# Low parts of weights made by an adding DMA instead of a VectorE subtraction, in a planned one-core residual block

## The chip, the cores and the metric

The kernel runs on one core of one Trainium2 chip. A core has a matrix engine (TensorE, "PE" in the profile, with its weight loads listed apart as "PEld"), VectorE ("DVE"), ScalarE ("ACT"), GpSimd ("POOL") and SyncE ("SP"). They run their own instruction queues, each in order, and wait for one another through semaphores; 16 DMA engines move data between the chip's memory and the core's SBUF. The metric is the device time of one execution in microseconds, the median of the runs.

## What is computed

One block of a hybrid encoder on a sequence of 1024 tokens of width 1024, all in float32. Cut to what matters:

```python
h = rms_norm(x, norm_mix_pre)
proj = h @ w_in                                # 1024 x 5376 weights
q, k, v = heads(proj[..., :1536])              # stick-breaking attention, 8 heads of 64
o_sb = stick_breaking_attention(q, k, v)
o_rw = rwkv7_time_mix(proj[..., 1536:3328])    # RWKV-7: token shift, LoRA, scan over time
gates = sigmoid(proj[..., 3328:] + b_gate)
merged = gates[..., :D] * (o_sb @ w_sb_out) + gates[..., D:] * (o_rw @ w_rw_out)
x = x + rms_norm(merged @ w_o, norm_mix_post)
h = rms_norm(x, norm_ffn_pre)
f = (silu(h @ w_ffn_gate) * (h @ w_ffn_up)) @ w_ffn_down
out = x + rms_norm(f, norm_ffn_post)
```

## The kernel before

**Products in three parts.** Large products run in a float32 format of PE that keeps fewer bits than float32 (`fp32r` in the profile). To keep the precision, each operand is split into a high part, which is the operand rounded to that format, and a low part, which is what the rounding left. A product is then high x high + high x low + low x high, three matmuls that add into one PSUM tile (`mm3`, line 606). For each block of 128 rows of the contraction the order is: weight high with activation high, weight high with activation low, weight low with activation high. So the low part of a weight is needed by the third matmul of its product.

**How a weight tile is made.** `weights` (line 599) loads a tile into a place of class `raw` with a DMA of SP's queue (`load`, line 589), takes a place each of classes `whi` and `wlo` (`parts`, line 594), and splits (`split`, line 602): ACT copies `raw` to the high part in the rounded format, and DVE subtracts the high part from `raw` into the low part. The classes `raw`, `whi` and `wlo` have two places each (lines 665 and 666), so that one tile can be prepared while another is in use. `split` also serves activations and the later stages; these call it without `weights`.

**Who calls `weights`.** `rwkv` (line 900) for 12 tiles of `w_in`; `gate_tiles` (line 799) for 16; `att_inputs` (lines 1187, 1198, 1214) for 12; `merge` (line 1308) for 16 tiles of `w_sb` and `w_rw`, half as large. The first 40 have 128 x 1024 elements and feed two products of 24 matmuls each (two halves of the sequence), the 16 have 128 x 512 and feed two of 12. The two tiles of `w_in` for the LoRA stage and those of `w_o` and the FFN are split elsewhere.

**Stages.** `norm_in` normalises and transposes the input, `lora` computes the small projections and spills three arrays per pair of heads, `rwkv` runs four pairs of heads in two halves each: elementwise work, an inversion of small triangular blocks on DVE (`rw_inverse`, a series of 31 steps), and a chain of 8 steps (`rw_chain`) in which PE, DVE, ACT and POOL take turns; POOL makes the tile `sp` of each step. `attention` runs 8 heads, with a mask by POOL, a scan by DVE and transposes by PE. `merge` multiplies with the output weights and the gates, which were spilled to memory and are loaded again (`b_mg`). `output` and `ffn` follow. Projections of later pairs and the gate tiles are filler work for PE: they have no partner that waits soon.

**The planner.** Nothing is issued as it is written. Every operation is recorded (`record`, line 321) with a cost in ns (`cost`, line 132) and with what it reads and writes, and `schedule` (line 414) then plays the machine: five engines, each taking the able operation of highest priority as soon as it is free, places of SBUF and PSUM granted in turn, and a delay from each operation to those that depend on it (`LATENCY`, line 248; 2030 ns and more after a DMA of SP). An operation's `late` (ns) is added to that delay. The order that comes out is issued engine by engine, and on the chip each engine keeps to it. So a change of one cost can move instructions on every engine.

**Issue.** In the profile nearly all instructions have line 586, where the planned operations are issued, so groups are told apart by their tiles: `whi_whi<-raw_raw` is the copy to the high part, `wlo_wlo<-raw_raw,whi_whi` the subtraction, `d_d<-big_h,whi_whi` a matmul of a projection into the PSUM class `d`. All DMAs go out on SP's queue. In a row of the profile a place taken over by another tile of its class can lend it its name (`b_sh`, `b_dg`, ...).

Of the kernel before, what the change touches and what calls it, by code (L numbers as in the profile page):

```python
# [7 lines left out]
F32R = mybir.dt.float32r  # L8
BF16 = mybir.dt.bfloat16
AF = mybir.ActivationFunctionType  # L10
ALU = mybir.AluOpType
# [5 lines left out]
S = 1024  # L17
# [62 lines left out]
def is_ap(x):  # L80
    return hasattr(x, "tensor") and hasattr(x, "offset") and hasattr(x, "ap")


def count(shape):
    n = 1
    for d in shape:
        n *= d
    return n
# [43 lines left out]
def cost(engine, method, kw, in_psum):  # L132

    out = kw.get("out", kw.get("ap"))
    if out is None:
        return 1283.0
    n = count(out.shape[1:])
    if engine == "tensor":
        if method == "transpose":
            return 2 + max(out.shape[0], n) / 1.2  # L140
        m, full = count(kw["lhsT"].shape[1:]), kw["lhsT"].dtype == F32
        if out.shape[0] <= CH and n <= CH:
            return 65.0 if out.shape[0] == CH else 20.0
        return 2 * (2 + max(m, n) / 1.2) if full else max(m / 2.4, 1.5 + 0.4435 * n)
    psum = any(is_ap(v) and k not in OUTS and in_psum(v) for k, v in kw.items())
    if engine == "vector":
        if method == "tensor_copy" and not psum:
            return 60 + 0.52 * n
        if method == "tensor_reduce":
            n = count(kw["in_"].shape[1:])  # L150
            return 64 + 1.042 * n
        if method == "scalar_tensor_tensor":
            return max(196, 68 + (1.16 if psum else 1.1) * n)
        if method == "tensor_tensor_scan":
            return 60 + 2.083 * n
        if method == "tensor_tensor" and abs(kw["in0"].ap[-1][0]) > 16:
            return 68 + 1.8 * n
        return 68 + 1.042 * n
    if engine == "scalar":
        extra = "accum_out" in kw or any(is_ap(kw.get(k)) for k in ("scale", "bias"))  # L160
        return 55 + 0.833 * n + (0 if psum else 40) + (90 if extra else 0)
    if engine == "gpsimd":
        if method == "memset":
            return 98 + 0.8 * n
        if method == "tensor_copy":
            return 180 + 3.4 * n
        if method == "tensor_scalar":
            return 320 + 2.4 * n
        return 150 + 2.1 * n
    size = 4 * count(out.shape)  # L170
    return max(450.0, size / 360.0)

SHORT_RUNS = 2200.0


HELD, HEAD = 115.0, 140.0
# [84 lines left out]
class Block:  # L263
# [54 lines left out]
    def in_psum(self, ap):  # L318
        return not str(ap.space).endswith("DRAM") and self.tiles[ap.offset // TSTRIDE - 1].cls.psum
# [277 lines left out]
        return hi, lo  # L597

    def weights(self, src, shape):
        return self.parts(self.load(src, shape), shape)  # L600

    def split(self, hi, lo, src):
        self.nc.scalar.copy(hi, src)
# [45 lines left out]
def hybrid_block(tc, x, xt, w_in, consts, params, rows, ups, gup, w_sb, w_rw, w_o, w_fg, w_fu, w_fd, out):  # L649
    b = Block(tc, {a.tensor.name for a in (x, xt, w_in, consts, params, rows, ups, gup, w_sb, w_rw, w_o, w_fg, w_fu, w_fd)})  # L650
    nc = b
    T = b.t
    with ExitStack() as es:
        b.open(es)
        b.cls("cst", 1, CC_TI)
        b.cls("par", 1, PC_N)
        b.cls("small", 4, 16)
        b.cls("tiny", 4, 4)
        b.cls("ss", 8, 4)
        b.cls("carry", 5, 1)  # L660
        b.cls("pl", 3, 8)
        b.cls("sp", 3, CH)
        b.cls("q", 4, 256)
        b.cls("big", 4, 4 * S)
        for n in ("raw", "whi", "wlo"):
            b.cls(n, 2, S)
        b.cls("b", NB, 1040, halves=True)
        for n, k in (("d", 2), ("e", 2), ("c", 2), ("y", 2)):
            b.cls(n, k, H, psum=True)

        cst, par = T("cst", [P, CC_TI]), T("par", [P, PC_N])

        one = T("q", [P, P])
        nc.gpsimd.memset(one, 1.0)
        b.zero = T("b", [P, H], BF16, "zero")
        nc.vector.memset(b.zero, 0.0)
        idle_products(b, AWAKE[0])

        b.xin, b.w_lora, b.xt = [], [], []
        def tokens(*ms):  # L680
            for m in ms:
                b.xin.append(T("b", [P, D], F32, "x"))
                nc.sync.dma_start(b.xin[m], x[m * P : m * P + P, :])
        def channels(t):
            for q in range(2):
                b.xt.append(T("b", [P, 4, TQ], F32, "xt"))
                nc.sync.dma_start(b.xt[-1], xt[t][:, 4 * q : 4 * q + 4, :])
        tokens(0)
        nc.sync.dma_start(cst[:, 0:P], consts[:, 0:P])
        tokens(1)  # L690
        nc.sync.dma_start(par, params)
        b.w_lora.append(b.load(w_in[24], [P, KT, P]))
        channels(0)
        b.w_lora.append(b.load(w_in[25], [P, KT, P]))
        tokens(2, 3)
        channels(1)
        tokens(4, 5)
        nc.sync.dma_start(cst[:, P:CC_TI], consts[:, P:CC_TI])
        channels(2)
        tokens(6, 7)  # L700
        channels(3)
        b.ident = cst[:, CC_ID : CC_ID + P]
        b.cen = cst[:, CC_CEN : CC_CEN + P]
        b.ones = cst[:, CC_ONE : CC_ONE + P]
        b.mask_a = cst[:, CC_MA : CC_MA + P]
        b.tinit = consts[:, CC_TI : CC_TI + 256]
        b.scanm = consts[:, CC_SC:CC_N]
        b.eps = T("small", [P, 2])
        nc.gpsimd.memset(b.eps[:, 0:1], RMS_EPS)
        nc.gpsimd.memset(b.eps[:, 1:2], GN_EPS)  # L710
        b.om = T("small", [P, 14])
        nc.gpsimd.tensor_scalar(out=b.om, in0=par[:, PC_MU : PC_MU + 14], scalar1=-1.0, scalar2=1.0, op0=ALU.mult, op1=ALU.add)
        b.oka = T("small", [P, 4])
        nc.gpsimd.tensor_scalar(out=b.oka, in0=par[:, PC_KA : PC_KA + 4], scalar1=-1.0, scalar2=1.0, op0=ALU.mult, op1=ALU.add)
        b.pc = lambda col: par[:, col : col + 1]

        b.gsc = [b.scratch([P, S], f"gsc{j}") for j in range(16)]
        b.orw_d = [b.scratch([P, S], f"orw{p}") for p in range(PAIRS)]
        b.x2_d = b.scratch([S, D], "x2d")
        b.w_in, b.w_sb, b.w_rw = w_in, w_sb, w_rw  # L720
        b.ngate = 0

        b.steady = STEADY[0]
        norm_in(b, one)
        lora(b, ups, gup)
        b.steady = STEADY[1]
        rwkv(b)
        b.steady = STEADY[2]
        attention(b)
        b.steady = STEADY[3]  # L730
        ms, sums = merge(b)
        b.steady = True
        output(b, x, w_o, rows, ms, sums)
        ffn(b, w_fg, w_fu, w_fd, rows, out)
        b.issue()


def idle_products(b, n, after=None):
    ps = b.t("y", [P, H])
    for i in range(n):  # L740
        b.tensor.matmul(ps, lhsT=b.zero[:, 0:P], rhs=b.zero, start=True, stop=True)
        if after:
            b.ops[-1].preds.add(after)
# [150 lines left out]
def rwkv(b):  # L894
    T = b.t
    b.table("natural_log_exp_and_others")
    carry = {}
    units = [[{}, {}] for p in range(PAIRS)]

    def project(p):  # L900
        for name, j in (("k", 4 + p), ("r", p), ("v", 8 + p)):
            w = b.weights(b.w_in[12 + j], [P, KT, P])
            for hf in range(2):
                ps = b.proj(w, hf)
                units[p][hf][name] = T("b", [P, H], F32, name)
                shifted(b, ps, carry, j, hf, units[p][hf][name])

    project(0)
    for p in range(PAIRS):
        for hf in range(2):  # L910
            rw_elementwise(b, units[p][hf], p, hf, b.spill[p][hf])
        if p + 1 < PAIRS:
            with Offset(b, PROJ):
                project(p + 1)
        gate_tiles(b, GATES_R[p])
        with Offset(b, CHAIN):
            for hf in range(2):
                rw_chain(b, units[p], p, hf)
                with Offset(b, POST):
                    rw_post(b, units[p][hf], p, hf, b.spill[p][hf])  # L920


def rw_elementwise(b, u, p, hf, spill):
# [95 lines left out]
    for at in ((hi, slice(None), lo), (lo, slice(None), hi)):  # L1019
        nc.sync.dma_start(xv[at], sv[at])  # L1020
        b.ops[-1].late = SHORT_RUNS

# [28 lines left out]
def rw_inverse(b, nd, nx, quads, tinit, p, hf):  # L1051
# [22 lines left out]
    nc.sync.dma_start(dt[:], td.rearrange("(c a) j k t -> (a j k) c t", a=4))  # L1074
    b.ops[-1].late = SHORT_RUNS

# [376 lines left out]
def ffn(b, w_fg, w_fu, w_fd, rows, out):  # L1453
    b.act = b.scratch([7, NFF // 2, P, H], "act")
    ffn_up(b, w_fg, w_fu)
    ffn_down(b, w_fd, rows, out)
# [324 lines left out]
```

## Time and profile before

| | us |
|---|---|
| median of 3 runs | 1591.97 |
| lowest and highest run | 1591.48, 1593.61 |
| the profiled execution | 1590.17 |
| its span, first to last instruction | 1588.1 |
| PE busy in it | 1563.3 |
| DVE busy | 1182.2 |
| ACT busy | 732.7 |
| POOL busy | 205.1 |

The granted TensorE clock is 0.999 over the span. The DMA engines moved 184.56 MB, 116 GB/s in the mean, all kernel transfers on one queue. "Busy" is the union of an engine's instructions; matmuls are pipelined and their ends modelled, so a PE that is busy is not thereby at its peak. A row of a group reads: line, engine, operation, out tile <- in tiles, shapes, count | busy us, mean ns of one | idle us of the engine just before them, and what ended most of it. A row of a wait reads: who waited <- for whom: us in total, times, longest. A row of a timeline: start and duration in us, engine, operation, tiles, count of merged instructions. A row of a DMA issue: tiles, queue, count, KB each, median us from issue to landing.

### The profile page before, as it was taken

The numbers are of one execution on the slowest core, as the hardware profiler recorded it, in microseconds if no ns is written. First come the engines' busy times: TensorE is split into PE (matmuls) and PEld (weight loads), VectorE is DVE, ScalarE is ACT, GpSimd is POOL, SyncE is SP. The second block draws the span as 40 slices with busy tenths as digits, with TensorE's granted clock in tenths as the row PEclk, the third lists the DMA queues.
The fourth block names the chain that finished last, engine by engine and source line by source line (L and its number), as shares of the span: only waits on it lengthen the run. The fifth ranks groups of instructions, "written<-read, shape, count | busy, mean of one in ns | idle before, by whom it ended". The sixth has DMA issues, their size and how long they took to land.

```text
span 1588.1 us, 23824 instructions
## 1 busy us (share of the span) xinstructions
PE 1563.3 (98%) x8829; PEld 1266.1 (80%) x8829; DVE 1182.2 (74%) x2134; ACT 732.7 (46%) x1437; POOL 205.1 (13%) x383
## 2 busy tenths in 40 slices
PE   8999999999999999999999999999999999999998
PEld 6877877777777888888788888888888888888886
DVE  7768789969874878896369799766666666877485
ACT  6733334452345766775445664332332332454352
POOL 1131233415232322230000000000000000000000
PEclk9999999999999999999999999999999999999999
DMA  7632332343321000003543522332232233874445
GB/s 302 226 105 82 85 102 71 84 120 93 99 74 41 27 28 27 28 21 113 193 139 106 184 108 74 99 113 100 86 113 100 91 118 124 302 247 145 141 151 185
DMA packets 108115, 184.56 MB, mean 116 GB/s; under 512 B 42464, under 2 KB 43744, under 8 KB 108000
## 3 DMA queue, kind: packets, MB, share of 16 engines
q1 hardware_dynamic: 108000, 183.05, 34.9%
q8 instruction: 69, 1.13, 0.3%
q14 instruction: 46, 0.38, 0.1%
HBM read 133.47 MB, written 47.45 MB: 114 GB/s over the span
## 4 chain that ended last, share of the span: by engine, by line
PE 87%; DVE 7%; issue 2%; DMA 2%; ACT 1%; SPq 1%; POOL 0%; DVEq 0%; POOLq 0%; ACTq 0%
PE d_d L586 40%; PE e_e L586 19%; PE c_c L586 16%; PE y_y L586 11%; DVE q_q L586 2%; DVE b_xt L586 1%; DVE b_bk L586 1%; DMA b_nl<-nd 1%; SPq L586 1%; DVE b_nx L586 0%; DVE wlo_wlo L586 0%; DVE big_h L586 0%; DVE b_sv L586 0%; DMA b_mg<-gsc 0%; DVE b_tmp L586 0%
## 5 line engine op out<-in xcount | busy, mean ns | idle before, releaser
L586 PE MATMUL d_d<-big_h,whi_whi 128*128 128x512 f32 x1312 | 443.7, 409 | 1.0 <-ACT b_upw L586 1.0
L586 PEld LDWEIGHTS d_d<-big_h,whi_whi 128*128 128x128 f32 x1312 | 239.8, 189 | 51.2 <-issue 6.7
L586 PE MATMUL d_d<-big_h,wlo_wlo 128*128 128x512 f32 x656 | 266.7, 407 | 0.1
L586 PEld LDWEIGHTS d_d<-big_h,wlo_wlo 128*128 128x128 f32 x656 | 123.7, 189 | 25.4 <-issue 2.2
L586 DVE TENSOR_TENSOR q_q<-b_nl,q_q 128x2 f32<-128x2 f32 (+30 forms) x248 | 87.0, 351 | 16.2 <-PE y_y L586 6.8
L586 ACT CAST whi_whi<-raw_raw 128x1024 fp32r<-128x1024 f32 (+1 forms) x58 | 53.8, 929 | 83.1 <-PE d_d L586 70.7
L586 DVE TENSOR_TENSOR_SCAN b_nb<-b_nb 128x128 f32<-128x128 f32 (+3 forms) x64 | 85.3, 1351 | 2.6 <-POOL b_nb L586 2.1
L586 DVE TENSOR_TENSOR wlo_wlo<-raw_raw,whi_whi 128x1024 fp32r<-128x1024 f32 (+1 forms) x58 | 62.5, 1077 | 26.4 <-ACT whi_whi L586 26.3
L586 POOL TENSOR_SCALAR sp_sp<-b_sv,pl_pl 64x64 f32<-64x64 f32 x120 | 60.0, 500 | 131.3 <-DVE b_sv L586 125.3
L586 ACT CAST b_wd<-b_wraw 128x512 fp32r<-128x512 f32 x70 | 42.0, 620 | 65.1 <-DVE b_wraw L586 30.8
L586 DVE TENSOR_REDUCE q_q<-q_q 128x1 f32<-128x2 f32 (+30 forms) x248 | 62.2, 251 | 7.0
L586 DVE TENSOR_TENSOR b_wd<-b_wraw,b_wd 128x512 fp32r<-128x512 f32 x70 | 46.2, 686 | 28.1 <-ACT b_wd L586 28.1
L586 PE MATMUL d_d<-b_wd,big_act 128*128 128x512 f32 x264 | 66.3, 393 | 0.0
L586 PE MATMUL e_e<-b_wd,big_act 128*128 128x512 f32 x264 | 66.2, 393 | 0.0
L586 PEld LDWEIGHTS d_d<-b_wd,big_act 128*128 128x128 f32 x264 | 49.5, 188 | 11.6
L586 PEld LDWEIGHTS e_e<-b_wd,big_act 128*128 128x128 f32 x264 | 49.6, 188 | 11.4
L586 POOL TENSOR_SCALAR_AFFINE_SELECT b_nb<-b_nb 128x128 f32<-128x128 f32 x64 | 40.3, 635 | 123.5 <-ACT b_nb L586 121.2
L586 DVE TENSOR_TENSOR b_wt<-c_c,b_wt 128x512 fp32r<-128x512 f32 (+2 forms) x96 | 50.3, 547 | 3.4 <-ACT b_wt L586 2.1
L586 ACT COPY b_xv<-c_c 64x64 f32<-64x64 f32 x64 | 13.3, 207 | 82.8 <-PE c_c L586 49.1
L586 PE MATMUL c_c<-b_wd,big_act 128*128 128x512 f32 x198 | 50.6, 394 | 0.0
L586 PE MATMUL y_y<-b_wd,big_act 128*128 128x512 f32 x198 | 50.6, 394 | 0.0
L586 ACT CAST b_wt<-c_c 128x512 fp32r<-128x512 f32 (+2 forms) x96 | 43.6, 480 | 12.7 <-PE c_c L586 11.5
(670 smaller groups left out, 3520.4 us busy)
## 6 DMA issues: line engine op xcount, KB each, us to landing
raw_raw<-w_in SPq DMA_DIRECT2D x42, 512.0 KB, 3.5
act<-b_u SPq DMA_DIRECT2D x46, 256.0 KB, 3.1
raw_raw<-w_fg SPq DMA_DIRECT2D x22, 512.0 KB, 3.5
raw_raw<-w_fu SPq DMA_DIRECT2D x22, 512.0 KB, 3.6
b_wraw<-w_fd SPq DMA_DIRECT2D x22, 512.0 KB, 5.5
b_x<-x SPq DMA_DIRECT2D x16, 512.0 KB, 6.0
b_mg<-gsc SPq DMA_DIRECT2D x28, 256.0 KB, 4.9
raw_araw<-act SPq DMA_DIRECT2D x14, 512.0 KB, 4.5
```

The source lines that it names most:

```text
L586: getattr(getattr(self.real, op.engine), op.method)(**kw)
```

## The change

`weights` no longer calls `split`. ACT reads the raw tile twice: it copies it to the high part as before, and copies it again, multiplied by -1, into the low part's place. That second result is rounded to the same format, so it is the negative of the high part. Then a DMA issued by POOL reads the weight once more from memory and adds it to what stands in the low part's place: weight minus high part. DVE has no share in it any more. The transfer is recorded with 4000 ns of `late`, a POOL DMA is priced at 1000 ns of POOL's time, and the class `wlo` gets a third place. The builder's argument `dynamic_dma_scratch_size`, left at its default before, is set to 2048.

```diff
@@ cost @@
     if engine == "gpsimd":
+        if method == "dma_start":
+            return 1000.0
         if method == "memset":
@@
 SHORT_RUNS = 2200.0
+LANDING = 4000.0
@@ weights @@
     def weights(self, src, shape):
-        return self.parts(self.load(src, shape), shape)
+
+        raw = self.load(src, shape)
+        hi, lo = self.t("whi", shape, F32R), self.t("wlo", shape, F32R)
+        self.nc.scalar.copy(hi, raw)
+        self.nc.scalar.activation(lo, raw, AF.Copy, scale=-1.0)
+        self.nc.gpsimd.dma_start(out=lo, in_=src, accum_op=ALU.add)
+        self.ops[-1].late = LANDING
+        return hi, lo
@@ hybrid_block @@
-        for n in ("raw", "whi", "wlo"):
-            b.cls(n, 2, S)
+        for n, k in (("raw", 2), ("whi", 2), ("wlo", 3)):
+            b.cls(n, k, S)
@@ kernel @@
-    nc = bacc.Bacc("TRN2", target_bir_lowering=False, num_devices=1)
+    nc = bacc.Bacc("TRN2", target_bir_lowering=False, num_devices=1, dynamic_dma_scratch_size=2048)
```

## The prediction

> **What bounds the kernel now.** I read the page's chain of work that ended last, then the busy time by stage, then who TensorE (PE) waited for. From the page:
>
> ```profile
> span 1588.1 us, 23824 instructions
> ...
> PE 87%; DVE 7%; issue 2%; DMA 2%; ACT 1%; SPq 1%; POOL 0%; DVEq 0%; POOLq 0%; ACTq 0%
> PE d_d L586 40%; PE e_e L586 19%; PE c_c L586 16%; PE y_y L586 11%; DVE q_q L586 2%; DVE b_xt L586 1%; DVE b_bk L586 1%; DMA b_nl<-nd 1%; SPq L586 1%; DVE b_nx L586 0%; DVE wlo_wlo L586 0%; DVE big_h L586 0%; DVE b_sv L586 0%; DMA b_mg<-gsc 0%; DVE b_tmp L586 0%
> ```
>
> The chain is PE for 87%. VectorE (DVE) has 7%, nearly all of it for other tiles: the instructions that the change removes, `DVE wlo_wlo`, round to 0%. Now five stretches of the span (columns: length, then busy us and instructions of PE, its weight loads, DVE, ACT, POOL, then clock, DMA share, GB/s); the stages in them are head and lora, rwkv, attention, merge, and the rest:
>
> ```profile
> 0.00:100.00 100.00, 92.19 (x474) 73.93 (x475) 68.13 (x110) 63.34 (x107) 16.27 (x47) 1.00 0.64 233
> 100.00:500.00 400.00, 392.09 (x3247) 307.53 (x3246) 322.62 (x868) 162.23 (x351) 127.89 (x246) 1.00 0.30 87
> 500.00:740.00 240.00, 239.30 (x1455) 203.92 (x1454) 198.87 (x273) 161.71 (x361) 60.92 (x91) 1.00 0.11 36
> 740.00:845.00 105.00, 103.51 (x450) 83.80 (x449) 54.49 (x87) 43.73 (x74) 0.00 (x0) 1.00 0.49 157
> 845.00:1588.10 743.10, 736.22 (x3210) 596.94 (x3208) 538.04 (x800) 301.72 (x545) 0.00 (x0) 1.00 0.40 136
> ```
>
> PE idles 7.9 us in the rwkv stage (400.00 - 392.09), 0.7 in attention, 1.5 in merge. That is a visible ceiling of 10.1 us, 0.6% of the span, on what any help to DVE in these stages can return; a matmul that takes long for another reason would not show as idle. The ceiling has one obvious weak place: in rwkv DVE is 81% busy (322.6 of 400).
>
> **The change, part by part.** What goes and what comes, from the groups by shape:
>
> ```profile
> L586 DVE TENSOR_TENSOR wlo_wlo<-raw_raw,whi_whi 128x1024 fp32r<-128x1024 f32 x42 | 51.5, 1227 | 17.9 <-ACT whi_whi L586 17.8
> L586 DVE TENSOR_TENSOR wlo_wlo<-raw_raw,whi_whi 128x512 fp32r<-128x512 f32 x16 | 11.0, 685 | 8.5 <-ACT whi_whi L586 8.5
> L586 ACT CAST whi_whi<-raw_raw 128x1024 fp32r<-128x1024 f32 x42 | 43.9, 1048 | 52.7 <-PE d_d L586 43.9 <-DVE q_q L586 4.7 <-DMA raw_raw<-w_fu 2.6
> L586 ACT CAST whi_whi<-raw_raw 128x512 fp32r<-128x512 f32 x16 | 9.9, 616 | 30.4 <-PE d_d L586 26.8 <-PE c_c L586 3.6
> ```
>
> Two of the 42 belong to the FFN, which does not call `weights`, so 40 + 16 tiles change. *Removed from DVE:* 40 x 1.227 + 16 x 0.685 = 60.0 us. How much of it lies in rwkv says the busy time of `wlo`'s instructions alone (the third busy time is that of DVE):
>
> ```profile
> 100.00:500.00 400.00, 150.89 (x371) 69.82 (x370) 28.20 (x23) 1.00 0.30 87
> ```
>
> That is 23 tiles, 28.2 us, so DVE falls there from 81% to 74% (294.4 of 400). *Added to ACT:* a second pass over the raw tile, which I price like the cast: 40 x 1.048 + 16 x 0.616 = 51.8 us. ACT is at 41% in rwkv, 67% in attention, 42% in merge, and takes it; only the lora stretch (below) has ACT full. *Added to the DMA engines:* 40 x 0.5 MB + 16 x 0.25 MB, about 25 MB, spread over stages where they are 11 to 64% busy. No PE instruction is added or removed.
>
> *Gain.* PE's named waits from 40 to 860 us begin:
>
> ```profile
> PE e_e L586 <- DVE b_nx L586: 3.3, 3, 1.8
> PE d_d L586 <- ACT b_mg L586: 1.5, 1, 1.5
> ```
>
> The other rows that name DVE are smaller. Of the three waits on `b_nx`, the longest has a removed instruction right in front:
>
> ```profile
> 405.89 1.23 DVE L586 TENSOR_TENSOR wlo_wlo<-raw_raw,whi_whi 128x1024 fp32r<-128x1024 f32 x1
> ...
> 407.11 0.68 DVE L586 TENSOR_TENSOR b_nx<-e_e,cst_cst 128x512 f32<-128x512 f32 x1
> ...
> 407.85 0.94 PE L586 MATMUL e_e<-cst_cst,b_dg 128*128 128x128 f32 x6 [1.80 <-DVE b_nx L586]
> ```
>
> Without the 1.23 us in front, `b_nx` starts earlier by that much. That is 1.2 us directly. A lighter DVE also shortens other steps of the rwkv chain; I take 2.0 us in all. Bounds: 0, if those steps then wait for PE, and 7.9, all of rwkv's idle.
>
> *Loss at the first projection.* Here the low part is used as it is made, with ACT and DVE both full:
>
> ```profile
> 39.00:47.00 8.00, 7.92 (x46) 6.58 (x46) 7.88 (x11) 7.69 (x13) 1.46 (x4) 1.00 0.21 69
> ```
>
> ```profile
> 39.59 1.99 ACT L586 CAST whi_whi<-raw_raw 128x1024 fp32r<-128x1024 f32 x2
> ...
> 42.02 1.22 DVE L586 TENSOR_TENSOR wlo_wlo<-raw_raw,whi_whi 128x1024 fp32r<-128x1024 f32 x1
> 42.12 1.09 PE L586 MATMUL d_d<-big_h,whi_whi 128*128 128x512 f32 x4
> ```
>
> The first low part is ready at 43.24, and PE, which has run four products that need only the high part, goes on at once. After the change the ACT pair can be high and low of the first tile (done at 41.6); then POOL issues, then the transfer lands. No DMA of POOL's is in this trace, nor one that adds. Issue, from POOL's rows:
>
> ```profile
> L586 POOL TENSOR_SCALAR sp_sp<-b_sv,pl_pl 64x64 f32<-64x64 f32 x120 | 60.0, 500 | 131.3 <-DVE b_sv L586 125.3
> ...
> L586 POOL TENSOR_TENSOR b_tt<-b_tt 128x512 f32<-128x512 f32 x1 | 2.2, 2197 | 3.3 <-DVE b_tt L586 3.3
> L586 POOL CAST b_b<-raw_raw 128x1024 fp32r<-128x1024 f32 x2 | 2.1, 1035 | 3.1 <-DMA raw_raw<-w_in 3.1
> ```
>
> Bounds 0.5 and 2.2 us; I take 1.0, by the cast, POOL's only work on a whole weight tile, which is also what the new line of the planner's cost says. Landing, from the page's issues and (last line) those of 24 to 50 us alone:
>
> ```profile
> raw_raw<-w_in SPq DMA_DIRECT2D x42, 512.0 KB, 3.5
> ...
> b_xt<-xt SPq DMA_DIRECT2D x8, 512.0 KB, 9.8
> ```
>
> ```profile
> raw_raw<-w_in SPq DMA_DIRECT2D x4, 512.0 KB, 6.3
> ```
>
> Bounds 3.5 (a plain load, to which adding can only add) and 9.8 (a crowded start). For the head I keep 3.5 to 6.3: the low part lands between 41.6 + 1.0 + 3.5 = 46.1 and 48.9. In between PE had used projection products to fill up. The busy time of that PSUM tile's instructions alone counts them:
>
> ```profile
> 43.10:46.20 3.10, 2.34 (x8) 1.23 (x7) 0.00 (x0) 0.00 (x0) 1.00 0.51 169
> 46.20:49.00 2.80, 1.44 (x6) 0.97 (x6) 0.00 (x0) 0.00 (x0) 1.00 0.65 159
> ```
>
> Seven (the eighth is the tail of the four) by 46.2, 13 by 49.0. At 0.229 us each (736.22 / 3210, the stage where PE runs without a break) PE loses 1.6 to 3.0 us, since nothing else was ready; I take 2.0. Zero is possible if lora's own products, one of whose splits on DVE stood behind the removed instruction, come forward to fill the hole.
>
> *Elsewhere the landing is covered.* One tile of rwkv and its first use:
>
> ```profile
> 365.48 1.21 DVE L586 TENSOR_TENSOR wlo_wlo<-raw_raw,whi_whi 128x1024 fp32r<-128x1024 f32 x1
> ...
> 380.62 0.39 PE L586 MATMUL d_d<-big_h,wlo_wlo 128*128 128x512 f32 x1
> ```
>
> The low part waits 13.9 us for PE there. Against that stand ACT 1.05, issue 1.0 and landing 3.5 to 6.3, less the 1.2 of DVE: hidden by the tile before it, and uncovered only if issue and landing together pass some 14 us. In merge the cover is thinner, one tile of 24 products, 5.5 us (24 x 0.229), but the third place for low parts lets the planner begin a tile earlier, which makes about 11; ACT 0.62, issue 1.0 and 3.5 fit twice. SP's queue loses and gains nothing; POOL's gains 56 issues, each of which first waits for ACT with all later POOL work behind it: `sp` (wanted by the rwkv chain) and the mask of attention (PE is 99.7% busy there). In its own row `sp` stood idle 131.3 us before 120 instructions, 1.1 us each, so an issue of 1.0 mostly falls into idle time. I count nothing.
>
> **Sum.** Against the profiled execution's 1590.17 us (span 1588.1 and 2.1 around it): -2.0 + 2.0 + 0 = 1590.2. The median of the runs is 1591.97, 1.8 above that execution; so **1592.0**, no change. What three rounds can tell apart is about 0.2%, 3.2 us.
>
> The same landing by a rule: the Trainium skill, page "DMA: Bandwidth & Descriptors", section "Anatomy of one DMA", gives a DMA issued from GpSimd a fit of 2.0 us plus its bytes at 436 GB/s, an estimate of 3.2 us for 0.5 MB. The head would then lose 1.5 us, and the sum would be 1591.5. The trace's own plain loads take longer than that, 3.5 us in the median and 6.3 in the crowded window, and the fit says nothing of adding; I stay with the rows.
>
> **Rivals.**
> - *DVE was the real limit of rwkv, and the head's hole is filled.* For it: DVE at 81%, the 1.80 us wait behind a removed instruction. Against it: that is one wait in three. It returns two thirds to three quarters of rwkv's 7.9, about 5.5: 1586.5. Chance 0.29.
> - *Nothing is gained, the head is paid.* DVE's freed time goes idle, since PE hands it work no sooner: +2.0, 1594.0. The change would then do what it says without helping. Chance 0.08.
> - *POOL's queue becomes the new wait (slower).* Place: the rwkv chain, where an accumulating issue stands before `sp`. It decides from an issue (with its wait for ACT) longer than the 1.1 us that `sp` has spare. At 2.2 plus an ACT pass of 1.05 the chain is late by 2.1 for each of 23 tiles, 49 us; PE has filler work for most of it, and if a sixth reaches PE (my choice between none and all), +8: 1600.0. Against it: POOL is 32% busy there. Chance 0.20. An issue could also be held up by what DVE runs beside it, by no more than that instruction's length:
>
> ```profile
> L586 DVE TENSOR_SCALAR b_tmp<-b_tmp,par_par,small_small 128x512 f32<-128x512 f32 x3 | 2.3, 753 | 0.0
> ```
>
>   An issue of 1.0 + 0.75 would pass the 1.1, but for one such neighbour among many, so the chance stays low. (The Trainium skill, page "SBUF — State Buffer", section "SBUF: two separate sides", states such a rule: a VectorE instruction in a two-port mode locks GpSimd out, and the descriptors of its DMAs wait. No run here shows it yet.)
> - *The adding transfer lands later than its cover (slower).* Place: merge, at its start above all, where ACT already kept PE waiting 1.5 us. It decides from a landing of 9.4 us (the 11 of cover less ACT's 0.62 and the issue's 1.0). At 9.8 some 14 tiles are short by 0.4 each, 5.6 us, and one tile at the start, with the thinner cover, by 9.8 + 1.6 - 5.5 = 5.9: +11.5, 1603.5. Against it: merge's DMA engines are half idle. Chance 0.12.
>
> **Numbers.** The forecast itself has 0.31, its own range 1589 to 1595 (gain and head each between their ends). With the second rival, within 0.2% is 0.39; faster by more is 0.29, slower by more 0.20 + 0.12 = 0.32. The range must reach into both sides: from 1585 (rwkv's idle all but gone) to 1604 (the second slower rival). Since the planner sets every engine's order anew with the new costs, a shift of a few microseconds in either direction is inside it and has no single place.
>
> **What would show it.** Right: no `DVE wlo_wlo` instruction left but the FFN's two; DVE in rwkv near 295 of 400 us, ACT up by 52 us, PE idle in rwkv 5 to 7 us, and 1.5 to 3 us of new PE idle between 42 and 50 us behind a transfer into `wlo`. Faster rival: rwkv's PE idle under 3 us. POOL rival: POOL's issues over 1.1 us, PE waits on chain tiles (`b_sv`, `b_xv`) up by several us. Landing rival: transfers into `wlo` of 8 us or more and PE waits for them in merge. I am wrong as a whole if PE's matmul time itself grows, or if PE's idle changes by over 10 us.

## The result, and the profile after

The changed kernel takes 1626.09 us (median of 4 runs, 1624.42 to 1630.1) against 1591.72 of the kernel before (4 runs). The ratio is 1.0221, its 95% interval 1.0209 to 1.0233: **slower by about 35 us** (35.2 by the ratio, 34.4 between the medians), where the prediction had no change and a range up to 1604. The profiled execution took 1626.0 us.

From the page of the changed kernel: span, busy times, DMA queues (packets, MB, share of 16 engines' span) and the chain that ended last.

```profile
span 1624.2 us, 23910 instructions
...
PE 1577.7 (97%) x8829; PEld 1272.6 (78%) x8829; DVE 1124.9 (69%) x2078; ACT 777.7 (48%) x1493; POOL 249.8 (15%) x439
...
q0 software_dynamic: 8064, 25.17, 9.3%
...
PE 77%; DVE 6%; DMA 5%; ACT 2%; issue 1%; SPq 1%; POOL 0%; DVEq 0%; ACTq 0%; POOLq 0%
...
L589 POOL DMA_DIRECT2D wlo_wlo<-w_in x40 | 35.7, 893 | 105.4 <-ACT wlo_wlo L589 94.8
...
raw_raw<-w_in SPq DMA_DIRECT2D x42, 512.0 KB, 3.6
wlo_wlo<-w_in POOLq DMA_DIRECT2D x40, 512.0 KB, 5.7
```

DVE lost 57 us of work (1182.2 before, 1124.9 now) and ACT gained 45 (732.7 before, 777.7 now). ACT's new pass alone is 52.3 us, 56 instructions of 0.934 in the mean; why the rest of its work came out some 7 us lower was not followed up. The span grew by 36.1 us. PE's busy time grew by 14.4 us although its 8829 matmuls are the same, and its idle time went from 24.8 us (1588.1 - 1563.3) to 46.5 (1624.2 - 1577.7). In the chain DMA rose from 2% to 5%. The queue q0 is new: POOL's adding transfers, 25 MB. An issue takes 0.89 us and a low part lands 5.7 us after it.

The stages again, each boundary moved by as much as the work at it is late (5.5, 33, 35 and 36 us, read from the first or last matmuls of a tile on either side). Columns as in the prediction's view of five stretches.

```profile
0.00:105.50 105.50, 91.61 (x453) 72.27 (x454) 57.68 (x98) 66.03 (x109) 17.50 (x49) 0.94 0.76 246
105.50:533.00 427.50, 405.78 (x3331) 317.09 (x3329) 299.70 (x853) 187.69 (x382) 145.06 (x273) 0.98 0.46 111
533.00:775.00 242.00, 240.82 (x1401) 204.20 (x1400) 185.57 (x260) 172.49 (x373) 74.22 (x103) 1.00 0.27 63
775.00:881.00 106.00, 103.43 (x444) 82.49 (x443) 44.87 (x71) 49.65 (x86) 13.01 (x15) 1.00 0.72 194
881.00:1624.20 743.20, 736.07 (x3209) 596.59 (x3207) 537.09 (x798) 301.82 (x545) 0.00 (x0) 1.00 0.39 135
```

Head and lora lost 5.5 us, rwkv 27.5, attention 2, merge 1, the rest nothing. In rwkv PE's idle time went from 7.9 to 21.7 us, and the granted clock from 1.00 to 0.98; in head and lora the clock is 0.94. DVE is at 70% there, where it was at 81%. So DVE was relieved where it was busiest, and the stage became longer.

Whom PE waited for in the changed kernel (waits in all, times, longest):

```profile
PE y_y L589 <- DVE q_q L589: 6.2, 4, 3.3
PE e_e L589 <- DVE b_dg L589: 4.8, 1, 4.8
PE c_c L589 <- ACT b_pp L589: 4.6, 1, 4.6
...
PE y_y L589 <- DVE b_xv L589: 2.7, 1, 2.7
PE d_d L589 <- DMA wlo_wlo<-w_in: 2.5, 1, 2.5
PE c_c L589 <- ACT b_cum L589: 2.4, 1, 2.4
```

Only one of these rows names the new transfer: 2.5 us, once, the hole at the first projection that the prediction had foreseen. The others name tiles of rwkv's chain. (`b_dg` is the start of the kernel and stood in the profile before as well, with 4.2 us.) What is late behind `b_pp` is to be seen in the timeline from 495 us on, of which these are the rows of SP's and POOL's DMA issues and of `b_pp`:

```profile
496.20 0.33 SPq L589 DMA_DIRECT2D raw_raw<-w_in  x1
496.54 0.91 POOL L589 DMA_DIRECT2D wlo_wlo<-w_in  x1 [1.35 <-ACT b_xv L589]
...
498.82 0.69 ACT L589 ACTIVATE b_pp<-d_d,par_par 128x512 f32<-128x512 f32 x1
...
499.54 0.33 SPq L589 DMA_DIRECT2D gsc<-b_pp  x1
499.57 0.90 POOL L589 DMA_DIRECT2D wlo_wlo<-w_in  x1
...
507.02 0.63 ACT L589 ACTIVATE b_pp<-b_tt 128x512 f32<-128x512 f32 x1 [6.80 <-DMA gsc<-b_pp]
...
507.71 1.22 PE L589 MATMUL c_c<-b_pp,cst_cst 128*128 128x512 f32 x1 [4.62 <-ACT b_pp L589]
```

ACT writes a gate's tile at 498.82, SP stores it at 499.54, and two adding transfers are issued around that. The store of 256 KB keeps its buffer until about 507, over 7 us; in the kernel before, the largest group of such stores between 65 and 505 us landed in 2.4:

```profile
gsc<-b_tmp SPq DMA_DIRECT2D x7, 256.0 KB, 2.4
```

ACT, whose next result goes into the same place, stands for 6.8 us, and PE behind it for 4.6. No reader of a low part is in this picture. Three more of PE's waits look alike:

```profile
65.32 0.69 ACT L589 ACTIVATE b_cum<-c_c,par_par 128x512 f32<-128x512 f32 x1 [3.26 <-DMA g_d<-b_cum]
...
248.29 0.69 ACT L589 ACTIVATE b_sh<-d_d,par_par 128x512 f32<-128x512 f32 x1 [8.48 <-DMA gsc<-b_sh]
...
250.01 0.34 PE L589 MATMUL y_y<-b_nx,b_xv 128*64 128x64 f32 x4 [2.73 <-DVE b_xv L589]
...
363.32 0.45 DVE L589 STREAM_TRANSPOSE q_q<-q_q 128x256 f32<-128x256 f32 x1 [9.57 <-DMA q_q<-td]
```

After the start of the kernel PE has five waits of 2.4 us or more: 2.5 for the low part, and 2.4 (`b_cum`), 2.7 (`b_xv`, which DVE makes after work that needs ACT's `b_sh`), 3.3 (`q_q`) and 4.6 (`b_pp`) behind a store of SP's queue, for `q_q` with its reload. That gave the first theory.

### The profile page after: what moved, and what is told of

Same layout as the page of the kernel before. It is cut to its first block, busy times and chain, and to the rows that moved or that the text cites. A ratio compares the mean times of both kernels' runs of the same rounds, so it can differ in the third digit from the quotient of the medians.

```text
span 1624.2 us, 23910 instructions
## 1 busy us (share of the span) xinstructions
PE 1577.7 (97%) x8829; PEld 1272.6 (78%) x8829; DVE 1124.9 (69%) x2078; ACT 777.7 (48%) x1493; POOL 249.8 (15%) x439
## 3 DMA queue, kind: packets, MB, share of 16 engines
q0 software_dynamic: 8064, 25.17, 9.3%
## 4 chain that ended last, share of the span: by engine, by line
PE 77%; DVE 6%; DMA 5%; ACT 2%; issue 1%; SPq 1%; POOL 0%; DVEq 0%; ACTq 0%; POOLq 0%
PE d_d L589 33%; PE e_e L589 18%; PE c_c L589 15%; PE y_y L589 10%; DVE q_q L589 2%; DMA td<-q_q 1%; DMA q_q<-td 1%; SPq L589 1%; DMA gsc<-b_sh 1%; DVE b_nx L589 1%; DMA nd<-b_nx 1%; DVE b_sv L589 1%; DMA b_nl<-nd 1%; DMA gsc<-b_pp 0%; DVE b_bk L589 0%
## 5 line engine op out<-in xcount | busy, mean ns | idle before, releaser
L589 PE MATMUL d_d<-big_h,whi_whi 128*128 128x512 f32 x1312 | 451.2, 413 | 0.0
L589 PEld LDWEIGHTS d_d<-big_h,whi_whi 128*128 128x128 f32 x1312 | 243.5, 191 | 49.3 <-issue 3.4
L589 DVE TENSOR_TENSOR_SCAN b_nb<-b_nb 128x128 f32<-128x128 f32 (+3 forms) x64 | 85.4, 1348 | 7.2 <-POOL b_nb L589 6.6
L589 DVE TENSOR_TENSOR b_wd<-b_wraw,b_wd 128x512 fp32r<-128x512 f32 x67 | 44.5, 686 | 29.5 <-ACT b_wd L589 29.5
L589 POOL TENSOR_SCALAR_AFFINE_SELECT b_nb<-b_nb 128x128 f32<-128x128 f32 x64 | 45.1, 708 | 110.5 <-ACT b_nb L589 105.4
L589 ACT ACTIVATE wlo_wlo<-raw_raw 128x1024 fp32r<-128x1024 f32 (+1 forms) x56 | 52.3, 934 | 2.4 <-DMA raw_raw<-w_rw 1.9
L589 POOL DMA_DIRECT2D wlo_wlo<-w_in x40 | 35.7, 893 | 105.4 <-ACT wlo_wlo L589 94.8
```

The costliest lines, as they stand in the source:

```text
L589: getattr(getattr(self.real, op.engine), op.method)(**kw)
```

## The experiments

**The theories.** *Engines:* the adding transfers occupy the 16 DMA engines, and the stores and reloads of SP's queue, on which rwkv's chain and its buffers hang, land later than the planner takes them to. *Landing:* what costs time is PE's wait for the low parts. *POOL's queue:* an entry that waits for ACT holds up POOL's other work. *ScalarE:* the second pass over each tile is what is missing to the chain. In the diffs, "after" is the changed kernel. Times are medians with their ratio to the kernel before, run beside them. That kernel's median lay between 1589.9 and 1591.7 us from one session to the next, so a difference between runs of two sessions is uncertain by up to 2 us.

**e1_off_path.** VectorE makes the low part as before; the negated copy and the adding DMA go to a tile that nothing reads.

```diff
-        hi, lo = self.t("whi", shape, F32R), self.t("wlo", shape, F32R)
-        self.nc.scalar.copy(hi, raw)
-        self.nc.scalar.activation(lo, raw, AF.Copy, scale=-1.0)
-        self.nc.gpsimd.dma_start(out=lo, in_=src, accum_op=ALU.add)
+        hi, lo = self.parts(raw, shape)
+        ex = self.t("ex", shape, F32R)
+        self.nc.scalar.activation(ex, raw, AF.Copy, scale=-1.0)
+        self.nc.gpsimd.dma_start(out=ex, in_=src, accum_op=ALU.add)
```

> The low part is made by VectorE as before. Beside it ScalarE's negated copy and the adding DMA of GpSimd go into a spare tile that nothing reads, so that every transfer and every issue of the change is there, and nobody waits for them. Engines theory (the adding transfers hold the DMA engines, other transfers land late and in-order engines wait for those): most of the loss stays, 1611 to 1630 us. Landing theory (PE and the plan suffer because the low part itself lands later than the 4.0 us of the plan): 1588 to 1597 us.

Measured 1623.37, ratio 1.0207 (1.0185 to 1.0228). Nearly the whole loss is there with nobody waiting for the transfer: in the trace POOL's issue waits for ACT to fill the spare tile, and nothing waits for the tile after that, also not ACT when it fills the place again. The landing theory falls for all but a few us.

**e2_plain_load.** The same order of instructions on every engine as after, but the DMA overwrites instead of adding.

```diff
-        self.nc.gpsimd.dma_start(out=lo, in_=src, accum_op=ALU.add)
+        self.nc.gpsimd.dma_start(out=lo, in_=src)
```

> As the changed kernel, but GpSimd's DMA is a plain load without the addition; the low part is then the weight itself, so the subtraction is left out of the computation. Order, queues and waits are those of the changed kernel. Engines theory: a packet of 4096 bytes takes about 160 ns instead of 328, the landing falls from 5.7 to about 4 us, and at least half of the loss goes, 1592 to 1609 us. Plan theory (ScalarE's second pass, GpSimd's queue and the new order cost the time): no change, 1621 to 1631 us.

Measured 1612.47, ratio 1.0126 (1.0106 to 1.0147): 13.6 us under after, in one order. That lies between the two ranges expected: the addition matters, and costs less than half of the loss. (The issue is shorter too, 0.58 us of POOL's time instead of 0.89.) The page has its queue as

```profile
q0 software_dynamic: 8064, 25.17, 5.3%
```

The same packets and bytes take 5.3% of the 16 engines' span (1611.0 us here) instead of 9.3%: 85.4 us of all of them instead of 151.1, or 3.4 and 6.0 us for each of the 25.17 MB. The packets of a tile of 512 KB (0.524 MB) thus take 1.8 us on each of the 16 engines when they copy, and 3.1 us when they add.

**e3_landing_6000.** After, with the planner told that low parts land 2 us later.

```diff
-LANDING = 4000.0
+LANDING = 6000.0
```

> The changed kernel planned with 6000 ns of landing instead of 4000, near the 5.7 us that the profile shows. Landing theory: the plan now keeps PE busy until the low part is there, and the loss falls by half or more, to 1592 to 1609 us. Engines theory: the delays of the other transfers are still unplanned; 1612 to 1635 us.

Measured 1615.64, ratio 1.0157 (1.0142 to 1.0172): 10.5 us come back. Not the bulk, as the engines theory had it.

**e4_act_pass_only.** ScalarE's negated copy stays, VectorE adds the weight to it, POOL issues nothing.

```diff
-        self.nc.gpsimd.dma_start(out=lo, in_=src, accum_op=ALU.add)
-        self.ops[-1].late = LANDING
+        self.nc.vector.tensor_tensor(out=lo, in0=raw, in1=lo, op=ALU.add)
```

> The changed kernel with ScalarE's negated copy and the third place for low parts, but VectorE adds the raw weight to it and no DMA of GpSimd is issued. What ScalarE's second pass, the third place and the smaller scratch cost alone. Engines theory and landing theory: like before, 1587 to 1598 us. Plan theory, as far as it lies in ScalarE's pass: 1605 us or more.

Measured 1600.29, ratio 1.0060 (1.0045 to 1.0075): 9 us without any new transfer, more than the engines and landing theories had allowed.

**e5_tiny_transfer.** As e1, but each adding DMA moves 4 of the tile's 128 partitions. Every engine keeps e1's order; POOL's 56 entries wait for ScalarE as they did there.

```diff
-        self.nc.gpsimd.dma_start(out=ex, in_=src, accum_op=ALU.add)
+        self.nc.gpsimd.dma_start(out=ex[0:4], in_=src[0:4], accum_op=ALU.add)
```

> As e1_off_path (VectorE makes the low part as before; ScalarE's negated copy goes into a spare tile that nobody reads), but the adding DMA of each tile moves only 4 of its 128 partitions, so POOL's queue still has 56 entries that wait for ScalarE and the data engines get almost nothing. Engines theory (the traffic delays the stores and loads of SP's queue): near e4_act_pass_only, 1597 to 1605. POOL-queue theory (the entry in POOL's queue, waiting for ScalarE, holds up POOL's other work): near e1_off_path, 1614 to 1624.

Measured 1597.94, ratio 1.0051 (1.0034 to 1.0068). The same instructions in the same order on every engine, with nearly all of the bytes gone: 25 us come back. This is the cleanest pair of the study. POOL's entries hardly changed (an issue takes 0.82 us here and 0.90 in e1, and POOL stood idle before the 40 large ones for 88.4 and 94.2 us), so POOL's queue isn't the cause of these 25 us, and the traffic is. The DMA issues of 65 to 520 us show whom the traffic hit; first e1, then e5:

```profile
ex_ex<-w_in POOLq DMA_DIRECT2D x27, 512.0 KB, 5.8
...
td<-q_q SPq DMA_DIRECT2D x32, 32.0 KB, 3.2
...
gsc<-b_tt SPq DMA_DIRECT2D x3, 256.0 KB, 5.7
```

```profile
td<-q_q SPq DMA_DIRECT2D x32, 32.0 KB, 2.0
...
gsc<-b_tt SPq DMA_DIRECT2D x3, 256.0 KB, 2.7
...
ex_ex<-w_in POOLq DMA_DIRECT2D x28, 16.0 KB, 2.8
```

The stores of the chain (`td`) went from 2.0 to 3.2 us, three of the gates' (`gsc<-b_tt`) from 2.7 to 5.7 (medians). These are among the groups that moved most. Taken one by one, in the order that both traces share, of the 219 transfers that SP issues in that stretch 37 land over 2 us later in e1, at most 4.6, and the median one 0.1. So most are as fast as before and some are much later; in the changed kernel itself the median of `td` is 2.0, as in the kernel before, and it is single stores that PE waits for. Whether they are held up in the DMA engines or at the memory behind them, these runs don't separate. And PE's waits, first e1, then e5:

```profile
PE y_y L589 <- DVE q_q L589: 8.0, 4, 4.4
PE e_e L589 <- DVE b_dg L589: 5.3, 2, 5.1
```

```profile
PE e_e L589 <- DVE b_dg L589: 4.9, 1, 4.9
PE y_y L589 <- DVE q_q L589: 2.4, 2, 1.5
```

`q_q`, which holds what comes back through `td`, kept PE waiting 8.0 us in e1 and 2.4 in e5.

**e6_places_only.** The kernel before with three places for low parts and the smaller descriptor scratch.

```diff
-        for n in ("raw", "whi", "wlo"):
-            b.cls(n, 2, S)
+        for n, k in (("raw", 2), ("whi", 2), ("wlo", 3)):
+            b.cls(n, k, S)
...
-num_devices=1)
+num_devices=1, dynamic_dma_scratch_size=2048)
```

> The kernel before with the third place for low parts and the smaller descriptor scratch, and nothing else: no pass on ScalarE, no DMA from POOL. If the 9 us of e4_act_pass_only come from the new plan that three places make: 1597 to 1602. If they come from ScalarE's extra pass: 1590 to 1594.

Measured 1591.40, ratio 1.0009 (1.0000 to 1.0018). The places and the scratch by themselves don't cost it.

**e7_sp_spare_load.** The kernel before with a second plain load of every tile, on SP's queue, that nobody reads, into three places of their own (and the smaller scratch).

```diff
+        ex = self.t("ex", shape)
+        self.nc.sync.dma_start(ex, src)
         return self.parts(self.load(src, shape), shape)
```

> The kernel before with a second plain load of each of the 56 weight tiles, on SP's queue, into a spare class of three places that nobody reads: traffic and SP issues alone, nothing on ScalarE or POOL. Engines theory: about the plain transfer's share, 1598 to 1608. POOL-queue theory and ScalarE theory: 1590 to 1595, as neither engine has more to do.

Measured 1606.04, ratio 1.0094 (1.0077 to 1.0112). Traffic costs 16 us here without POOL and without ScalarE. e2 stood 21 above its kernel before, 8 to 9 of which e4 and e5 have without traffic, so 12 to 13 there. The order is another one (see the scatter below), and SP's own queue has 56 entries more, whose part was not tried apart.

**e8_not_in_rwkv.** After, but rwkv's own projections and the gates keep VectorE's subtraction.

```diff
-            w = b.weights(b.w_in[26 + j], [P, KT, P])
+            w = b.weights(b.w_in[26 + j], [P, KT, P], add=False)
...
-            w = b.weights(b.w_in[12 + j], [P, KT, P])
+            w = b.weights(b.w_in[12 + j], [P, KT, P], add=False)
```

> The changed kernel with the new way only for the weight tiles of attention's inputs and of merge (28 of 56); the tiles of rwkv's own projections and of the gates keep VectorE's subtraction, so that the first projection, lora and most of rwkv have no adding DMA. If the loss arises where stores and reloads through DRAM feed the rwkv chain (all theories that place it in rwkv): 1591 to 1600. If each adding DMA costs alike, wherever it stands: half of the loss stays, 1606 to 1612.

Measured 1599.50, ratio 1.0055 (1.0037 to 1.0072). The range is that of the theories that place the loss in rwkv. But its page has `q0 software_dynamic: 4032, 10.49, 4.1%`, 42% of the bytes; by bytes alone 15 us would be left, and 10 are. The 5 between them are within what a new plan alone does (below), so the run fits and doesn't decide.

**e9_plan_late.** As e3, and the planner takes every transfer of SP's to need 4.0 us in place of 2.0.

```diff
-    "sync": {"tensor": 2030, "vector": 2030, "scalar": 2030, "gpsimd": 2060, "sync": 2030},
+    "sync": {"tensor": 4030, "vector": 4030, "scalar": 4030, "gpsimd": 4060, "sync": 4030},
```

> As e3_landing_6000, but the planner also takes every transfer of SP's queue to land 4.0 us after its issue instead of 2.0, so that it orders the engines' work and the places for buffers for late stores and reloads. Engines theory, with the harm coming from waits on late stores and reloads that the plan did not foresee: 1599 to 1610. If the plan cannot make up for it (the work between a store and its reload is fixed by the chain): 1612 to 1625.

Measured 1595.10, ratio 1.0033 (1.0020 to 1.0046), below the range expected: some 30 us of the 35 are back, by two numbers of the plan and with every byte still moved. Its page and its DMA issues of 65 to 520 us:

```profile
q0 software_dynamic: 8064, 25.17, 9.5%
```

```profile
wlo_wlo<-w_in POOLq DMA_DIRECT2D x27, 512.0 KB, 6.8
gsc<-b_sh SPq DMA_DIRECT2D x8, 256.0 KB, 3.5
```

and whom PE waited for:

```profile
PE e_e L589 <- DVE b_dg L589: 5.2, 1, 5.2
PE d_d L589 <- DVE b_kst L589: 3.2, 1, 3.2
PE d_d L589 <- DVE b_dg L589: 2.1, 1, 2.1
```

The transfers are as slow as in after (9.5% against 9.3%, `gsc<-b_sh` 3.5 us against 3.4, low parts even 6.8), but PE no longer waits for `b_pp` or `b_xv`, and for `q_q` only 0.4 us. The delay of the stores costs time where the order of the work does not allow for it.

**e10_no_vector_op.** As e4 without VectorE's addition.

```diff
-        self.nc.vector.tensor_tensor(out=lo, in0=raw, in1=lo, op=ALU.add)
```

> As e4_act_pass_only, with VectorE's addition left out, so that the low part of each weight is the negated weight itself (the subtraction of the high part is left out of the computation): what VectorE's relief is worth with no transfer beside it. By the prediction's first term, 2.0 us of gain over e4: 1598; its bounds 0 to 7.9 give 1592 to 1600. A relief worth nothing: 1600; one that makes up for ScalarE's pass: 1590 to 1592.

Measured 1595.68, ratio 1.0033 (1.0020 to 1.0047): 4.6 us under e4, inside the prediction's bounds for the relief.

**e11_pool_pass.** The kernel before with a negated copy made by POOL, that nobody reads; no DMA.

```diff
+        ex = self.t("ex", shape, F32R)
+        self.nc.gpsimd.tensor_scalar(out=ex, in0=raw, scalar1=-1.0, scalar2=None, op0=ALU.mult)
```

> The kernel before with the negated copy of each weight made by POOL in place of ScalarE, into a spare tile that nobody reads, and no DMA from POOL. If the 8 to 9 us of e4 and e5 are ScalarE's (its queue feeds the chain of rwkv): 1590 to 1594. If any pass of about 1 us over each weight tile, holding its place for longer, costs the same: 1597 to 1601.

Measured 1609.92, ratio 1.0124 (1.0107 to 1.0141), outside both. The group's row shows why it doesn't answer the question:

```profile
L589 POOL TENSOR_SCALAR ex_ex<-raw_raw 128x1024 fp32r<-128x1024 f32 x40 | 117.7, 2943 | 82.6 <-DMA raw_raw<-w_in 80.3 <-DVE q_q L589 1.7
```

The pass takes POOL 2.94 us, not the 1 us I had reckoned with, and sits in front of `sp`. It says nothing on ScalarE.

**e12_half_packets.** After, with each adding DMA in two halves.

```diff
-        self.nc.gpsimd.dma_start(out=lo, in_=src, accum_op=ALU.add)
-        self.ops[-1].late = LANDING
+        h = shape[1] // 2
+        for k in (slice(0, h), slice(h, 2 * h)):
+            self.nc.gpsimd.dma_start(out=lo[:, k], in_=src[:, k], accum_op=ALU.add)
+            self.ops[-1].late = LANDING
```

> The changed kernel with each adding DMA cut into two, over half of the columns each, so that its packets are half as long (2048 bytes for w_in) and twice as many, the bytes being the same. If a store's packets stand each behind one packet of the adding transfer: the store is held up half as long, 1612 to 1620. If the engine's total time for the bytes counts: 1622 to 1632. POOL's second issue (some 0.9 us for each tile) should cost nothing by e5_tiny_transfer.

Measured 1613.75, ratio 1.0149 (1.0134 to 1.0164), 12 us under after, though its 16128 packets take 10.1% of the engines. It fits stores that stand behind one packet at a time; but the plan is another too, and e16 (below) doesn't bear it out.

**e13_before_late.** The control for e9: the same figure of 4.0 us in the kernel before (e9's last diff alone).

> The kernel before, its planner told that SP's transfers land 4.0 us after their issue instead of 2.0; nothing else. If e9_plan_late cured a harm of the adding transfers: 1588 to 1596, no better than before. If that figure makes a better plan for any kernel, by the 20 us that it gave between e3 and e9: 1570 to 1582.

Measured 1595.22, ratio 1.0029 (1.0019 to 1.0039). The figure is no better plan in general: it costs the kernel before 4.5 us. So e9 cured something that the change had brought, and with it the change stands level with its control, as far as two plans can be compared: 1595.10 and 1595.22.

**e14_sync_late_only.** After with the figure for SP's transfers, the landing left at 4.0.

> The changed kernel with the planner's figure for SP's transfers at 4.0 us, and the low part's own landing left at the change's 4.0 us. If the late stores and reloads of SP's queue carry most of the loss: 1596 to 1608. If it takes the later landing too: 1612 to 1622.

Measured 1605.94, ratio 1.0094 (1.0077 to 1.0110). With e3 and e9 this makes a square: after 1626.1, landing alone -10.5, SP's figure alone -20.2, both -31.0 (9.8, 19.1 and 29.5 when each run is taken against its own kernel before). The two add up within the scatter of plans (below), and about two thirds come back by the figure for SP's transfers, which the change does not touch.

**e15_act_late.** e4 with the figure of 4.0 us.

> As e4_act_pass_only (ScalarE's negated copy, VectorE's addition, no DMA from POOL) with the planner's figure for SP's transfers at 4.0 us. If ScalarE's 8 to 9 us are held up by stores and buffers that the plan takes to be free too soon: 1590 to 1595. If ScalarE's time itself is short in rwkv: 1597 to 1603.

Measured 1601.11, ratio 1.0072 (1.0050 to 1.0094). Nothing here says that the 9 us of e4 are late stores; but the figure alone cost the kernel before 4.5 us (e13), and the scatter of plans is of this size.

**e16_late_half.** e9 with e12's halves.

> As e9_plan_late with each adding DMA cut into two halves, as in e12_half_packets. If what is left of e9 is still stores behind adding packets: 1588 to 1593. If the plan has covered that already: 1593 to 1597, as e9.

Measured 1594.02, ratio 1.0020 (1.0011 to 1.0029): 1 us under e9, the best of all versions with the change, and still not faster than before.

**e17_half_3030 and e18_before_3030.** e16 and e13 with 3.0 us instead of 4.0.

> As e16_late_half with the planner's figure for SP's transfers at 3.0 us instead of 4.0. If the harm is that stores land later than planned, halved packets (stores in 3 to 4 us) are nearly covered by 3.0 and the pessimism costs less: 1589 to 1594. If 3.0 leaves waits uncovered: 1595 to 1601. Under 1588 would be a gain by the change that the runs so far do not show.

> The kernel before with the planner's figure for SP's transfers at 3.0 us, nothing else: the control for e17. Between before (1590.7) and e13 (1595.2): 1590 to 1594.

Measured 1600.00, ratio 1.0055 (1.0043 to 1.0068), and 1598.01, ratio 1.0042 (1.0028 to 1.0055). The control missed its range: 3.0 us is worse for the kernel before than either 2.0 or 4.0. This is **the scatter of plans**. The kernel before, in four plans with nothing added to its work, stands at 0 (as it is), +1.5 (e6), +4.5 (e13) and +7 us (e18). Three new plans are few, so the scatter may be wider. A difference of up to some 7 us between two kernels whose instructions are ordered differently can't be put down to a mechanism. The pairs e1 and e5, and after and e2, have one order each and stand outside this doubt; the 20 and 31 us of e14 and e9 are well above it; the 8 to 9 of e4 and e5, the 4.6 of e10 and half packets are not.

**The clock.** PE's busy time grew with no matmul added. The windows of the changed kernel around two of the stalls:

```profile
46.60:49.40 2.80, 0.64 (x2) 0.20 (x2) 2.57 (x5) 2.75 (x6) 0.00 (x0) 0.99 0.54 107
49.40:52.80 3.40, 3.08 (x7) 2.48 (x8) 1.73 (x2) 0.69 (x2) 0.00 (x0) 0.50 0.61 231
500.00:506.70 6.70, 3.08 (x15) 2.08 (x14) 0.78 (x3) 0.21 (x1) 1.44 (x4) 1.00 0.83 174
506.70:513.50 6.80, 5.79 (x14) 4.08 (x15) 1.60 (x5) 3.23 (x7) 1.41 (x2) 0.50 0.01 2
```

Behind both stalls the granted clock is 0.50, for 3.4 and 6.8 us. There are six such periods in the changed kernel before its tail. The first, from 8 to 15 us, follows the wait at the start of the kernel and cost nothing to be seen: over the first 20 us PE is busy 13.24 us here and 13.29 in the kernel before, with 54 matmuls each. e6, which has no added transfer, has one there too. The other five are 23.9 us together, so at most 12 us of lost PE time, of the 14.4 by which its busy time grew; the rest is not traced. A store that lands 5 us late can thus cost PE its wait and then up to 3.4 us more. The profile before has no such period ahead of its tail. But not every wait halves the clock: in e1 two waits of 2.5 to 2.6 us, ending at 205.0 and 440.5, have a clock of 1.00 behind them. How much of the loss comes through the clock was not tried apart.

## Why the prediction was wrong, step by step

- **The step that failed: "Added to the DMA engines".** It put 25 MB on engines "11 to 64% busy", priced them at nothing, and concluded that "SP's queue loses and gains nothing". Some 25 us of the 35 are this term, by e1 against e5, in e1's order. Two things were missed. A mean share of 30% says nothing about one store that starts within an adding transfer, whose packets take 3.1 us of each engine for a tile (from e2's numbers above): single stores landed up to 4.6 us later (e1 against e5). And SP's transfers have little slack: the order is worked out with 2.0 us for each (2.2 more for two kinds), so the delay is paid wherever a chain or a buffer hangs on the store. e9 shows that second half: the same traffic, planned for, cannot be told from its control.
- **Where the prediction looked instead.** Both slower rivals were about the new transfer's own queue and its own landing. *POOL's queue* decided from an issue, with its wait for ACT, over 1.1 us. The issue took 0.89 us (at most 1.04), but POOL stood idle for ACT 94.8 us before 40 of them, 2.4 each, so its condition was met, and of its signs PE's waits on `b_sv` and `b_xv` rose (3.3 and 2.7 us). It isn't the cause all the same: e5 keeps the entry and its wait and loses the cost. *The landing in merge* decided from 9.4 us; none there took over 7.8, and merge lost 1 us. The mechanism that acted was in no rival, so the range ended at 1604.
- **The head's hole: right in place, about right in size.** Foreseen 1.6 to 3.0 us between 42 and 50 us behind the low part; the wait was 2.5, ending at 49.7. The landing was longer than its bounds, 7.6 us for this one tile against 3.5 to 6.3, and the half clock behind the hole was not reckoned with.
- **"Elsewhere the landing is covered": nearly right.** No other wait for a low part is among PE's. But the order was worked out with 4.0 us where the landing took 5.7, and telling the planner 6.0 gives 10.5 us (e3), just above the scatter; what else than PE's one wait hung on it is not shown.
- **DVE's relief: right as an amount of work, without return.** DVE is busy 299.7 us in rwkv (foreseen 294.4); the share fell to 70% where 74 were foreseen because the stage became longer. By itself the relief brought 4.6 us (e10 against e4), within the bounds of 0 to 7.9 and within the scatter.
- **"ACT takes it": open.** The pass was priced right (51.8 us foreseen, a mean of 0.934 by 56 is 52.3). e4, e5 and e15 stand 8 to 11 us above before with it, one at a time no more than the plans' scatter, but all three on the same side. Its share of the 35 us is open.
- **The test named there held:** "wrong as a whole if PE's matmul time itself grows, or if PE's idle changes by over 10 us". Both happened, +14.4 and +21.7.

By the runs, the 35 us are some 25 of traffic in an order planned without it (e1 against e5), a part of up to 9 that the new plan and ScalarE's pass share, and the head's wait of 2.5. That 13.6 us hang on adding instead of copying is from the other pair with one order, after against e2. The shares come from different orders, so their sum is good to a few us. That even a plan made for the transfers does not bring the change under the kernel before is shown for the two figures tried (e9, e16 and e17 at 1594 to 1600), not for all plans.

## What to carry to other kernels

A transfer on a queue of its own is not free because the engines are idle on average: look for the short stores and reloads on which a chain or a buffer hangs, and ask what each of them costs when it lands some microseconds later. Where an order is planned from fixed latencies, a change that alters the latencies of others needs them remeasured, and a second control with the same new figure in the old kernel. And before a few microseconds are given a cause, replan the old kernel with nothing changed but a figure of the planner, and see how far it moves.

## What the runs showed of the hardware that was not expected

- The packets of a DMA that adds into SBUF take nearly twice as long as those of one that copies: 9.3% against 5.3% of the span for the same 8064 packets, 3.1 us against 1.8 of each engine for a tile of 512 KB. It lands in 5.7 us; the plain transfers of the same tiles need 4.3 on POOL's queue (e2) and 3.6 on SP's.
- Transfers issued by POOL delay those issued by SP although they are in different queues (37 of SP's 219 transfers between 65 and 520 us land over 2 us later in e1 than in e5; the median one hardly moves). The Trainium skill, page "DMA: Bandwidth & Descriptors", section "Issuing engines are not separate DMA queues", says that DMAs run on the same 16 engines and interleave, whichever engine started them. The trace agrees.
- A wait of 2.5 us was enough to halve PE's clock for 3.4 us (49.4 to 52.8). The Trainium skill, page "TensorE: Matmul & The Clock Gate", section "What's actually happening", has the clock fall after an idle window of about 3.4 us; here a shorter gap sufficed, while two of 2.5 us in e1 and the 4.2 us at the start of the kernel before did not halve it (clock 1.00 over the first 100 us). So the length of a wait alone does not decide it here.
- POOL needs 2.94 us to negate a tile of 128x1024, where its cast of the same tile in the profile before took 1.04.
